# Masks of four attention heads on VectorE, their first inputs loaded earlier, and another share-out of the last additions and stores

## The chip, the cores and the metric

One core of a Trainium2 chip. The metric is the device time of one execution in microseconds, the median of several runs. The core has five engines that each work through their own list of instructions in order: TensorE (PE) multiplies matrices, VectorE (DVE), ScalarE (ACT) and GpSimd (POOL) work on tiles in on-chip memory, and SyncE (SP) issues transfers. ACT and POOL can issue transfers too. All matrices are fp32; a product is made of three passes over "high" and "low" parts (`whi`/`wlo`, `h_hi`/`h_lo`) so that little precision is lost.

## What is computed

One layer of a hybrid decoder for a prompt of 512 tokens with 16 learned ones in front, and for 8 sequences that decode 4 tokens each over 512 cached positions in pages of 128. D_MODEL is 2048, there are 8 heads of 128.

```python
h = rmsnorm(x, g_pre)
q, k, v, ga, cb, cc, ch, gc, ma, mc = split(h @ w_in)
a = stick_breaking(q, k, v) * silu(ga)
u = cc * ch
c = cb * causal_conv(u_ext) * silu(gc)
merged = sigmoid(ma + b_ga) * (a @ w_pa) + sigmoid(mc + b_gc) * (c @ w_pc)
y = x + rmsnorm(merged @ w_out, g_post)

# stick_breaking, per head; mask[t, s] = (s < t)
z = q @ k.T * SCALE + b_sb
log_keep = where(mask, log_sigmoid(-z), 0)
after = reverse_cumsum(log_keep) - log_keep
attn = where(mask, exp(log_sigmoid(z) + after), 0)
out = attn @ v
```

## The kernel before

The work runs in this order: norm and transposes; q, k and v and four heads (0 to 3, `head_now`); the decode scores over the key pages; the other columns of w_in (the "gates" loop over j and w); then the products with w_pc, in a loop over 16 column blocks j, about 1194 to 1350 us; then w_pa (from 1370 us), w_out, and the end (`rows`, `finish`). A weight block arrives by SP's queue as `raw`, ACT casts it to `whi`, DVE makes `wlo`.

Heads 4 to 7 (`head_here`) are attended inside the w_pc loop, at j = 0, 3, 6 and 9, so that their chain of small steps lies between products of w_pc. A head's scores z are computed with keys on partitions, in three groups of tiles (A: 128 x 512, B and C: 128 x 416). For each group ACT makes |z|, Exp, Ln and Relu (`softplus_parts`), DVE adds them up into r (L408 to L411), a mask sets r to 0 where the key isn't before the query, ACT and DVE split r (`hi`/`lo`, L423/L424), and PE adds the sums over later keys onto z (L593: `neg_u` is the triangle of -1, `neg_one` a full block). Then ACT takes Exp (e, L597), e is masked and split, and PE multiplies it by v (L603: `o`). DVE multiplies o by the gate (`gated`, L1034) and it is split into `a_hl`, the input of w_pa.

The masks are POOL instructions (`affine_select`, L550), ten a head: five on r, five on e. POOL also issues transfers in its own order: the value pages of the decode (`vpage`, L636), and in the w_pc loop the store of each gated product (L1064: `gate_scr <- gt`), followed by the loads of those gates for the w_pa stage (L1081: `gt <- gate_scr`). Loads of L1081 reuse the buffers that the stores of L1064 read.

The decode's value products (L747: `tp <- vpage`) are spread by `dec_step` over the gates and the w_pc loop; each is a matmul of 128 x 32 by 128 x 512, for one of four column quarters of a PSUM bank, and behind eight sequences' worth of them come transposes (L755) and additions (L760).

At the end `rows` turns the last columns of w_out into token rows (L1141, L1144), ACT squares them, DVE applies g_post; `finish` makes the factor `rs` and adds og * rs to x: for every row group four pieces of 512 columns, of which DVE does some (L1169), while for the others ACT scales (L1171) and POOL adds (L1172). All stores are SP's (L1174). Row group 4 has 32 rows. `finish` runs twice: for row groups 0 and 1 before the last products, for 2, 3 and 4 behind them.

The order of instructions on each engine is set when the program is built: a scheduler simulates a timeline and places the instructions by it. A change of one engine's work thus moves others.

Of the kernel before, what the change touches and what calls it, by code (L numbers as in the profile page):

```python
# [17 lines left out]
P = 128  # L18
# [34 lines left out]
LNEXP = "natural_log_exp_and_others"  # L53
SCALE = P ** -0.5
GATE_Q, GATE_K, GATE_V, GATE_GA = 0, 1024, 2048, 3072
COL_CB, COL_CC, COL_CH, COL_GC, COL_MA, COL_MC = 4096, 5120, 6144, 7168, 8192, 10240
# [3 lines left out]
def hybrid_step_kernel(  # L60
# [340 lines left out]

    def softplus_parts(e, l, r, t, src, bias, neg_bias=None):

        act.activation(e, src, AF.Abs, bias=bias)
        act.activation(e, e, AF.Exp, scale=-1.0)
        act.activation(l, e, AF.Ln, bias=one_c[:e.shape[0]])
        act.activation(r, src, AF.Relu, bias=bias)
# [3 lines left out]
        dve.tensor_add(r, r, t)  # L411


    d3ctx, hctx, nctx = (ExitStack() for _ in range(3))
    z_all = dp.tile([P, NPG, DB, H, DT], F32, name="z_all")
# [105 lines left out]

    def attend(pl, h, khi, klo, vhi, vlo, qr, pl_a=None):

# [22 lines left out]
        def mask(x, g):  # L546
            for st, c0, n, ts, m in tiles_of(g):
                w = min(st * P + m - ts, n)
                if w > 0:
                    pool.affine_select(out=x[:m, c0:c0 + w], in_=x[:m, c0:c0 + w], pattern=[[1, w]],  # L550
                                       compare_op=ALU.is_gt, fill=0.0, base=ts - st * P, channel_multiplier=-1)

        rs_, sp_, sf_ = {}, {}, {}
        for g in GROUPS:
# [28 lines left out]
        ot = o_ps()  # L583
        dve.memset(ot, 0.0)
        for g in GROUPS:
# [37 lines left out]
    def head_later(h):  # L623
# [3 lines left out]
        dec_step(2, "part")  # L627


    page_reg = {}  # L630
# [7 lines left out]
    def decode_steps():  # L638
# [3 lines left out]
        for said, part in (("part", units[:DEC1]), ("logits", units[DEC1:])):  # L642
            with tc.tile_pool(name="dec1", bufs=2, side="right") as d1:
                for hf, b in part:
# [7 lines left out]
                    for pg in range(NPG):  # L652
# [17 lines left out]
                        yield  # L670
            yield said
        BHT = DB * H * DT

# [54 lines left out]
        for g in range(2):  # L728
            for hf in range(2):
                cs = slice(hf * 512, (hf + 1) * 512)  # L730
                po = t_ps()
                for pg in range(NPG + 1):
                    if pg < NPG:
                        vts = []
                        for j in range(4):
                            vt = d3.tile([P, 512], F32, name="vpage", bufs=8)
                            page_load(vt, vc, 4 * g + j, pg, cs)
                            vts.append(vt)
                        if g + hf + pg == 0:
                            yield "values"  # L740
# [269 lines left out]
    a_hl = tok.tile([P, KD, TQ], F32R, tag="B", name="a_hl")  # L1010
    hl = cctx.enter_context(tc.tile_pool(name="headin", bufs=1))
# [3 lines left out]
    def head_loads(h):  # L1015
        kr = hl.tile([P, T], F32, name="kr")
        nc.sync.dma_start(kr, k_scr[h])
        qr = hl.tile([P, PQ], F32, name="qr")
        nc.sync.dma_start(qr, qt_scr[h][:, 0:PQ])
        vn = hl.tile([P, 5, P], F32, name="vn")  # L1020
        nc.sync.dma_start(vn[:, 0:4, :], vn_scr[h][0:512].rearrange("(a p) d -> p a d", p=P))
        nc.sync.dma_start(vn[0:16, 4, :], vn_scr[h][512:TP])
        return kr, vn, qr

    loaded = head_loads(NOW)
    for k in range(0, 8, 2):
# [15 lines left out]
    def head_here(h):  # L1042
        kr, vn, qr = loaded if h == NOW else head_loads(h)
        ot = attend(cp, h, *k_split(cp, kr), *v_split(cp, vn), qr, cp2)
        gated(h, ot, sg_load(h)[:, 0, 0:PQ])
# [20 lines left out]
    split_evac(a_hl[:, 0:8, PQ:TQ], a_hl[:, 8:16, PQ:TQ], sg_s, sg_s)  # L1066
    d3ctx.close()
    dctx.close()
    cctx.close()
# [50 lines left out]
    with tc.tile_pool(name="outp", bufs=1) as op:  # L1120
        ogr = op.tile([REST, D - CW], F32, name="ogr")

        def og_rest(cs):

            return og_a[:REST, 4 * D + cs.start:4 * D + cs.stop] if cs.stop <= CW else \
                ogr[:, cs.start - CW:cs.stop - CW]

# [8 lines left out]
        def rows(j, ii, tb, g, rest):  # L1136
# [6 lines left out]
            if rest:  # L1143
                pe.transpose(out=pt[:REST, n:n + P], in_=tb[:, ROWS[4][0]:ROWS[4][0] + REST], identity=ident)  # L1144
            for b, i in enumerate(ii):
# [3 lines left out]
            if rest:  # L1149
                square(4, j, pt[:REST, n:n + P], REST)  # L1150
                dve.tensor_mul(og_rest(cs), pt[:REST, n:n + P], g[:REST])

        def finish(ii, npool):

# [4 lines left out]
            with tc.high_priority():  # L1159
                dve.reduce_sum(s1, ssq[:, ii[0]:ii[-1] + 1, :], axis=mybir.AxisListType.X)  # L1160
                rstd_of(dve, rs, s1, tmp, P, w)
            for b, i in enumerate(ii):
                n = ROWS[i][1]
                for c in range(4):
                    cs = slice(c * CW, (c + 1) * CW)
                    og = og4[:n, i, cs] if i < 4 else og_rest(cs)
                    xc, r = xs_[i][:n, cs], rs[:n, b:b + 1]
                    if c < 4 - npool[b]:
                        dve.scalar_tensor_tensor(out=xc, in0=og, scalar=r, in1=xc, op0=ALU.mult, op1=ALU.add)  # L1169
                    else:  # L1170
                        act.activation(og, og, AF.Copy, scale=r)  # L1171
                        pool.tensor_add(xc, xc, og)  # L1172
                    for p0, p1, dst in outs[i]:
                        nc.sync.dma_start(dst[:, cs], xc[p0:p1])  # L1174

# [56 lines left out]
        xa = tok.tile([P, 4, D], F32, tag="A", name="xa")  # L1232
        xs_ += [xa[:, i, :] for i in range(3)]
        parts = [((0, n, xp[t0:min(t0 + n, PQ), :]),) for t0, n in ROWS]
# [3 lines left out]
        outs[3] = ((0, np_, yp[t0:PQ, :]), (np_, P, ys))  # L1238
        for i in range(5):
            load_rows(xs_[i], parts[i])  # L1240

        finish((0, 1), (1, 1))
        both = []
# [3 lines left out]
        for m in range(2):  # L1247
# [4 lines left out]
            rows(j + m, (2, 3), cols[m], g[:, m], True)  # L1252
        finish((2, 3, 4), (1, 1, 2))
    mctx.close()
# [25 lines left out]
```

## Time and profile before

| | |
|---|---|
| median of 3 runs | 1661.16 us (1659.37 to 1664.0) |
| profiled execution | 1663.13 us, its span 1661.5 us |
| PE busy | 1600.6 us (96% of the span) |
| DVE, ACT, POOL busy | 1252.6, 974.8, 262.7 us |
| granted PE clock, mean | 0.981 |

Busy time is the time in which an engine executes an instruction; waits and the issue of transfers are left out. The span is what the profile covers, and the time of that execution is 1.6 us longer. Where PE is busy for nearly all of the span, the places with idle time or with a granted clock below 1 are few, and they are read from windows of 5 us. In a row of the timeline stand the start, the duration, the engine, the line, the operation with what it writes and reads, the count, and in brackets how long the engine had been idle and what ended that.

### The profile page before, as it was taken

The page shows a single profiled execution, that of the slowest core. Times are in us where ns is not written, and L with a number is a line of the kernel's source. Part 1 is how long each engine was busy: PE and PEld are TensorE (multiplying, and loading weights), DVE is VectorE, ACT ScalarE, POOL GpSimd, SP SyncE. Part 2 cuts the span into 40 slices and gives each one's busy share as a digit, 9 for nine tenths or more (in the row PEclk, how much of TensorE's full clock was granted, in tenths as well). Part 3 has the DMA queues.
Part 4 walks back from the last instruction along what each step waited for, and adds up shares of the span by engine and source line. Part 5 has one row for each costly group of instructions (what it writes and reads, how often), then busy time and mean ns, then how long its engine had stood idle before and what let it go on. Part 6 is the DMA issues. An engine that isn't in the chain of part 4 may idle for free. (4 is left out here: it accounts for less than half of the span.)

```text
span 1661.5 us, 31640 instructions
## 1 busy us (share of the span) xinstructions
PE 1600.6 (96%) x12174; PEld 1540.7 (93%) x12174; DVE 1252.6 (75%) x1669; ACT 974.8 (59%) x2532; POOL 262.7 (16%) x460
## 2 busy tenths in 40 slices
PE   7999999999999999999999999899999979999995
PEld 6999999999999999999999999888878969999995
DVE  4538888797979898988878888865466647877775
ACT  6247887746765656565667677953445533445552
POOL 0033233222101010000011011031232210000002
PEclk7999999999999999999999999999999989999998
DMA  9255545435544444444455454355895535433335
GB/s 225 77 177 155 155 144 160 143 119 171 174 131 128 128 134 129 129 133 134 135 157 170 148 166 143 103 185 163 283 317 169 170 99 174 154 111 94 94 105 193
DMA packets 307468, 252.72 MB, mean 152 GB/s; under 512 B 11569, under 2 KB 276853, under 8 KB 306213
## 3 DMA queue, kind: packets, MB, share of 16 engines
q1 hardware_dynamic: 279269, 161.90, 34.0%
q0 software_dynamic: 28016, 88.80, 16.3%
q8 instruction: 95, 1.56, 0.4%
q14 instruction: 56, 0.46, 0.1%
q10 hardware_dynamic: 32, 0.01, 0.0%
HBM read 217.95 MB, written 32.71 MB: 151 GB/s over the span
## 5 line engine op out<-in xcount | busy, mean ns | idle before, releaser
L235 ACT CAST whi<-raw 128x1024 fp32r<-128x1024 f32 x251 | 262.8, 1049 | 259.7 <-PE o L849 74.3
L236 DVE TENSOR_TENSOR wlo<-raw,whi 128x1024 fp32r<-128x1024 f32 x251 | 306.1, 1220 | 75.6 <-ACT whi L235 57.4
L849 PE MATMUL mm<-h_hi,whi 128*128 128x272 f32 (+1 forms) x1152 | 333.9, 290 | 6.2 <-ACT whi L235 6.2
L849 PE MATMUL mm<-h_lo,whi 128*128 128x272 f32 (+1 forms) x1152 | 332.4, 289 | 0.0
L849 PE MATMUL mm<-h_hi,wlo 128*128 128x272 f32 (+1 forms) x1152 | 332.0, 290 | 0.0
L849 PE MATMUL o<-t_hi,whi 128*128 128x272 f32 (+1 forms) x864 | 253.7, 294 | 7.4 <-DVE c L875 3.0
L849 PE MATMUL o<-t_hi,wlo 128*128 128x272 f32 (+1 forms) x864 | 251.2, 291 | 1.3 <-DVE wlo L236 1.3
L849 PE MATMUL o<-t_lo,whi 128*128 128x272 f32 (+1 forms) x864 | 251.2, 291 | 0.0
L236 DVE TENSOR_TENSOR wlo<-s,whi 128x1024 fp32r<-128x1024 f32 x126 | 154.0, 1222 | 101.3 <-ACT whi L235 101.0
L849 PEld LDWEIGHTS mm<-h_hi,whi 128*128 128x128 f32 x1152 | 217.4, 189 | 10.8 <-ACT whi L235 7.8
L849 PEld LDWEIGHTS mm<-h_lo,whi 128*128 128x128 f32 x1152 | 216.8, 188 | 2.5 <-issue 2.5
L849 PEld LDWEIGHTS mm<-h_hi,wlo 128*128 128x128 f32 x1152 | 216.4, 189 | 2.8 <-issue 2.5
L664 ACT ACTIVATE junk<-pr 128x128 f32<-128x128 f32 x592 | 182.7, 309 | 29.2 <-DVE pr L658 13.4
L235 ACT CAST whi<-s 128x1024 fp32r<-128x1024 f32 x126 | 131.6, 1045 | 100.1 <-PE o L849 32.2
L251 PE MATMUL mm<-h_hi,whi 128*128 128x280 f32 (+1 forms) x640 | 187.1, 293 | 0.0
L251 PE MATMUL mm<-h_hi,wlo 128*128 128x280 f32 (+1 forms) x640 | 187.1, 293 | 0.0
L251 PE MATMUL mm<-h_lo,whi 128*128 128x280 f32 (+1 forms) x640 | 186.7, 292 | 0.0
L849 PEld LDWEIGHTS o<-t_hi,whi 128*128 128x128 f32 x864 | 164.2, 190 | 16.5 <-issue 5.0
L849 PEld LDWEIGHTS o<-t_hi,wlo 128*128 128x128 f32 x864 | 164.4, 190 | 2.3 <-DVE wlo L236 2.2
L849 PEld LDWEIGHTS o<-t_lo,whi 128*128 128x128 f32 x864 | 164.9, 191 | 0.0
L658 DVE TENSOR_TENSOR pr<-kpage,qb 128x1024 f32<-128x1024 f32 x128 | 152.2, 1217 | 7.7 <-DMA kpage<-in_cache_k 3.4
L251 PEld LDWEIGHTS mm<-h_hi,whi 128*128 128x128 f32 x640 | 120.5, 188 | 0.7
(384 smaller groups left out, 3436.2 us busy)
## 6 DMA issues: line engine op xcount, KB each, us to landing
raw<-in_w_in SPq DMA_DIRECT2D x192, 512.0 KB, 4.2
kpage<-in_cache_k POOLq DMA_DIRECT2D x64, 256.0 KB, 3.4
qb<-q_scr POOLq DMA_DIRECT2D x32, 512.0 KB, 5.5
vpage<-in_cache_v POOLq DMA_DIRECT2D x64, 256.0 KB, 5.7
raw<-in_w_out SPq DMA_DIRECT2D x32, 512.0 KB, 4.0
gate_scr<-g POOLq DMA_DIRECT2D x32, 272.0 KB, 3.4
gt<-gate_scr POOLq DMA_DIRECT2D x16, 544.0 KB, 4.1
raw<-in_w_pc SPq DMA_DIRECT2D x16, 512.0 KB, 7.2
```

Of the source, the lines that this page charges most:

```text
L235: act.copy(hi, x)
L236: dve.tensor_sub(lo, x, hi.bitcast(F32))
L251: pe.matmul(o, lhsT=w, rhs=r[:, t0:t1], start=(k == 0 and n == 0), stop=(k == nk - 1 and n == 2))
L658: dve.tensor_mul(pr, kt.unsqueeze(1).broadcast_to([P, 2, 512]), qt))
L664: act.activation(junk, pr[:, t, h * P:(h + 1) * P], AF.Copy, accum_out=z_all[:, pg, b, 4 * hf + h, 2 * i + t:2 * i + t + 1])
L849: pe.matmul(o, lhsT=l[:, k, :], rhs=r, start=(start and k == 0 and m == 0), stop=(stop and k == 7 and m == 2), skip_group_check=True)
```

## The change

1. For heads 4 to 7 the masks become DVE instructions: min(x, BIG) times a 0/1 tile `after`, in place. The softplus instructions of the three groups are issued on ACT one group after the other in a fixed order, ahead of the sums. `o` is zeroed on ACT instead of DVE.
2. The inputs of head 4 (kr, qr, vn) are loaded in the gates loop, in a pool of their own; `vpage` has 7 buffers instead of 8.
3. At the end the 32 rows of group 4 lie as a tile of 128 x 512 (four column quarters below one another), their factor is spread over 128 partitions by a small matmul, and all additions are DVE's, mostly in pieces of 1024 columns. Stores alternate between SP's and ACT's queues: 4 in the first `finish` (8 before), 10 in the last (16 before).

```diff
-    def softplus_parts(e, l, r, t, src, bias, neg_bias=None):
-
-        act.activation(e, src, AF.Abs, bias=bias)
...
+    def softplus_acts(e, l, r, src, bias, pin=lambda ins: ins):
+        pin(act.activation(e, src, AF.Abs, bias=bias))
+        pin(act.activation(e, e, AF.Exp, scale=-1.0))
+        pin(act.activation(l, e, AF.Ln, bias=one_c[:e.shape[0]]))
+        pin(act.activation(r, src, AF.Relu, bias=bias))
...
-                if w > 0:
+                if w > 0 and after is not None:
+                    xm = x[:m, c0:c0 + w]
+                    dve.scalar_tensor_tensor(out=xm, in0=xm, scalar=BIG, in1=after[:m, ts - st * P:ts - st * P + w],
+                                             op0=ALU.min, op1=ALU.mult)
+                elif w > 0:
                     pool.affine_select(out=x[:m, c0:c0 + w], in_=x[:m, c0:c0 + w], pattern=[[1, w]],
...
         for g in GROUPS:
-            zt = gt[g]
-            e, l, r, t = tl("e", g), tl("l", g), tl("r", g), tl("lo", g)
-            softplus_parts(e, l, r, t, zt, b)
+            elr[g] = tl("e", g), tl("l", g), tl("r", g)
+            if after is not None:
+                softplus_acts(*elr[g], gt[g], b, pin)
+        for g in GROUPS:
+            (e, l, r), t = elr[g], tl("lo", g)
+            if after is None:
+                softplus_acts(e, l, r, gt[g], b)
+            softplus_sums(e, l, r, t)
             mask(r, g)
...
-        dve.memset(ot, 0.0)
+        if after is None:
+            dve.memset(ot, 0.0)
+        else:
+            act.copy(ot, zero_c.broadcast_to([P, PQ]))
...
-                            vt = d3.tile([P, 512], F32, name="vpage", bufs=8)
+                            vt = d3.tile([P, 512], F32, name="vpage", bufs=7)
...
+            if j + w == 14:
+
+                after = hl[0].tile([P, P], F32, name="after")
+                dve.tensor_scalar_add(after, neg_u.bitcast(F32), 1.0)
+                loaded = head_loads(NOW)
...
-        def finish(ii, npool):
+        def finish(ii, cuts):
...
+            queues = cycle((nc.sync, act))
             for b, i in enumerate(ii):
-                n = ROWS[i][1]
+                if i == 4:
+                    continue
+                for c0, c1 in zip(cuts[b], cuts[b][1:]):
+                    xc = xs_[i][:, c0:c1]
+                    dve.scalar_tensor_tensor(out=xc, in0=og4[:, i, c0:c1], scalar=rs[:, b:b + 1], in1=xc,
+                                             op0=ALU.mult, op1=ALU.add)
+                    p0, p1, dst = outs[i][0]
+                    next(queues).dma_start(dst[:, c0:c1], xc[p0:p1])
...
+            if ii[-1] == 4:
+                r4 = t_ps()[:, 0:1]
+                pe.matmul(r4, lhsT=to4.rearrange("p a b -> p (a b)"), rhs=rs[:REST, w - 1:w], start=True, stop=True)
+                r4s = op.tile([P, 1], F32, name="r4s")
+                act.copy(r4s, r4)
+                dve.scalar_tensor_tensor(out=xs_[4], in0=ogr, scalar=r4s, in1=xs_[4], op0=ALU.mult, op1=ALU.add)
+                dst = outs[4][0][2]
                 for c in range(4):
...
-                    if c < 4 - npool[b]:
-                        dve.scalar_tensor_tensor(out=xc, in0=og, scalar=r, in1=xc, op0=ALU.mult, op1=ALU.add)
-                    else:
-                        act.activation(og, og, AF.Copy, scale=r)
-                        pool.tensor_add(xc, xc, og)
-                    for p0, p1, dst in outs[i]:
-                        nc.sync.dma_start(dst[:, cs], xc[p0:p1])
+                    next(queues).dma_start(dst[:, c * CW:(c + 1) * CW], xs_[4][c * REST:(c + 1) * REST])
...
-        finish((2, 3, 4), (1, 1, 2))
+        finish((2, 3, 4), ((0, D // 2, D), (0, D // 2, 3 * CW, D)))
```

In the order of the instructions this shows at three places. Up to the w_pc loop every engine's order is the same but for a few rows. First POOL at the end of the heads, before (r and e are head 7's; `gt` a gate tile):

```order
L550 AFFINE_SELECT rA<-rA 128x112
L1064 DMA gate_scr<-gt 128x544
L1081 DMA gt<-gate_scr 128x1088 x2
L550 AFFINE_SELECT r<-r 128x128
L550 AFFINE_SELECT r<-r 16x16
L1064 DMA gate_scr<-gt 128x544
L1081 DMA gt<-gate_scr 128x1088
L550 AFFINE_SELECT r<-r 128x128 x2
```

POOL there with the change:

```order
L667 DMA vpage<-in_cache_v 128x512
L1089 DMA gate_scr<-gt 128x544 x9
L1107 DMA gt<-gate_scr 128x1088
L1089 DMA gate_scr<-gt 128x544
L1107 DMA gt<-gate_scr 128x1088
L1089 DMA gate_scr<-gt 128x544
L1107 DMA gt<-gate_scr 128x1088 x14
```

The masks have left the queue, and the gate loads have only gate stores around them. Second, PE at head 7, from the last products onto z to the first products with v, before:

```order
L593 MATMUL z<-lo,neg_u 128x144
L593 MATMUL z<-hi,neg_one 128x16
L593 MATMUL z<-lo,neg_one 128x16
L593 MATMUL z<-e,neg_one 128x400
L603 MATMUL o<-hi,vhi 128x400
L603 MATMUL o<-lo,vhi 128x400
```

PE there with the change (of the rows between `e,neg_one` and `hi,vhi` the last ones are shown; they are 35 matmuls of w_pc, which go on from z's last one):

```order
L252 MATMUL mm<-c_hl,whi 128x272 x2
L252 MATMUL mm<-c_hl,wlo 128x272
L252 MATMUL mm<-c_hl,whi 128x272
L624 MATMUL o<-hi,vhi 128x400
L252 MATMUL mm<-c_hl,whi 128x272
L252 MATMUL mm<-c_hl,wlo 128x272
L252 MATMUL mm<-c_hl,whi 128x272 x2
L252 MATMUL mm<-c_hl,wlo 128x272
L624 MATMUL o<-lo,vhi 128x400
```

Before, the o products follow z's directly and w_pc is used up by then; now products of w_pc stand between them. Third, PE at the decode's value products beside the first head of the loop, before:

```order
L251 MATMUL mm<-c_hl,whi 128x272
L593 MATMUL z<-loA,neg_u 128x512
L251 MATMUL mm<-c_hl,whi 128x272
L755 MATMUL tp<-ident,ob 128x128 x4
L251 MATMUL mm<-c_hl,wlo 128x272
L747 MATMUL tp<-vpage,z_all 32x512 x4
L593 MATMUL z<-hi,neg_u 128x400
```

PE beside the second head of the loop with the change (soon after its first product of `lo` onto z):

```order
L252 MATMUL mm<-c_hl,wlo 128x272
L779 MATMUL tp<-vpage,z_all 32x512
L252 MATMUL mm<-c_hl,whi 128x272
L779 MATMUL tp<-vpage,z_all 32x512
L252 MATMUL mm<-c_hl,whi 128x272
L252 MATMUL mm<-c_hl,wlo 128x272
```

Where four and more value products stood together, many now stand alone between products of w_pc and the steps of a head. Over the whole program the 64 of them form 31 runs before and 39 with the change.

More of the change, by code (lines that the diff above doesn't have):

```diff
@@ L411, in softplus_parts @@
         dve.tensor_add(r, r, t)
-    d3ctx, hctx, nctx = (ExitStack() for _ in range(3))
+    def softplus_parts(e, l, r, t, src, bias):
+        softplus_acts(e, l, r, src, bias)
+        softplus_sums(e, l, r, t)
+    d3ctx, hlctx, hctx, nctx = (ExitStack() for _ in range(4))
+    hl = []
     z_all = dp.tile([P, NPG, DB, H, DT], F32, name="z_all")
@@ L520, in v_proj, with attend @@
         return v_split(pl, vn)
-    def attend(pl, h, khi, klo, vhi, vlo, qr, pl_a=None):
+    def attend(pl, h, khi, klo, vhi, vlo, qr, pl_a=None, after=None):
         qhi = pl.tile([P, T], F32R, name="qhi")
@@ L627, in head_later, with head_loads @@
         dec_step(2, "part")
+    def head_loads(h):
+        kr = hl[0].tile([P, T], F32, name="kr")
+        nc.sync.dma_start(kr, k_scr[h])
+        qr = hl[0].tile([P, PQ], F32, name="qr")
+        nc.sync.dma_start(qr, qt_scr[h][:, 0:PQ])
+        vn = hl[0].tile([P, 5, P], F32, name="vn")
+        nc.sync.dma_start(vn[:, 0:4, :], vn_scr[h][0:512].rearrange("(a p) d -> p a d", p=P))
+        nc.sync.dma_start(vn[0:16, 4, :], vn_scr[h][512:TP])
+        return kr, vn, qr
     page_reg = {}
@@ L671, in decode_steps @@
             yield said
+        hl.append(hlctx.enter_context(tc.tile_pool(name="headin", bufs=1, side="right")))
         BHT = DB * H * DT
@@ L1043, in head_here @@
         kr, vn, qr = loaded if h == NOW else head_loads(h)
-        ot = attend(cp, h, *k_split(cp, kr), *v_split(cp, vn), qr, cp2)
+        ot = attend(cp, h, *k_split(cp, kr), *v_split(cp, vn), qr, cp2, after)
         gated(h, ot, sg_load(h)[:, 0, 0:PQ])
@@ L1067, in hybrid_step_kernel @@
     d3ctx.close()
+    hlctx.close()
     dctx.close()
@@ L1120, in hybrid_step_kernel @@
     with tc.tile_pool(name="outp", bufs=1) as op:
[L1121 to L1126, printed above, removed]
+        ogr = op.tile([P, CW], F32, name="ogr")
+        to4 = op.tile([REST, 4, REST], F32, name="to4")
+        dve.tensor_copy(to4, ident[:REST, :REST].unsqueeze(1).broadcast_to([REST, 4, REST]))
         ssq = og_a[:, 4 * D + CW:4 * D + CW + 5 * KD].rearrange("p (i j) -> p i j", j=KD)
@@ L1143, in rows @@
             if rest:
-                pe.transpose(out=pt[:REST, n:n + P], in_=tb[:, ROWS[4][0]:ROWS[4][0] + REST], identity=ident)
+                pr = t_ps()[:REST, :P]
+                pe.transpose(out=pr, in_=tb[:, ROWS[4][0]:ROWS[4][0] + REST], identity=ident)
             for b, i in enumerate(ii):
@@ L1149, in rows @@
             if rest:
-                square(4, j, pt[:REST, n:n + P], REST)
-                dve.tensor_mul(og_rest(cs), pt[:REST, n:n + P], g[:REST])
-        def finish(ii, npool):
+                square(4, j, pr, REST)
+                r0, c0 = j // 4 * REST, j % 4 * P
+                dve.tensor_mul(ogr[r0:r0 + REST, c0:c0 + P], pr, g[:REST])
+        def finish(ii, cuts):
             w = len(ii)
@@ L1161, in finish @@
                 rstd_of(dve, rs, s1, tmp, P, w)
+            queues = cycle((nc.sync, act))
             for b, i in enumerate(ii):
[L1163 to L1174 removed]
+                if i == 4:
[6 more added lines that the diff above has]
+                    next(queues).dma_start(dst[:, c0:c1], xc[p0:p1])
+                for p0, p1, dst in outs[i][1:]:
+                    next(queues).dma_start(dst, xs_[i][p0:p1])
+            if ii[-1] == 4:
[5 more added lines that the diff above has]
+                dst = outs[4][0][2]
+                for c in range(4):
+                    next(queues).dma_start(dst[:, c * CW:(c + 1) * CW], xs_[4][c * REST:(c + 1) * REST])
         def x_room(tag):
@@ L1232, in hybrid_step_kernel @@
         xa = tok.tile([P, 4, D], F32, tag="A", name="xa")
-        xs_ += [xa[:, i, :] for i in range(3)]
+        xs_ += [xa[:, 0, :], xa[:, 1, :], xa[:, 2, :CW]]
         parts = [((0, n, xp[t0:min(t0 + n, PQ), :]),) for t0, n in ROWS]
@@ L1238, in hybrid_step_kernel @@
         outs[3] = ((0, np_, yp[t0:PQ, :]), (np_, P, ys))
-        for i in range(5):
+        for i in range(4):
             load_rows(xs_[i], parts[i])
-        finish((0, 1), (1, 1))
+        for c in range(4):
+            nc.sync.dma_start(xs_[4][c * REST:(c + 1) * REST], parts[4][0][2][:, c * CW:(c + 1) * CW])
+        finish((0, 1), ((0, D // 2, D),) * 2)
         both = []
```

18 lines of the change are left out of this document (4 added, 14 removed).

## The prediction

> **What bounds the kernel now.** I read the page first, then the waits of PE.
>
> ```profile
> span 1661.5 us, 31640 instructions
> PE 1600.6 (96%) x12174; PEld 1540.7 (93%) x12174; DVE 1252.6 (75%) x1669; ACT 974.8 (59%) x2532; POOL 262.7 (16%) x460
> ```
>
> PE is busy for 96% of the span, so a change can pay in three ways only: it fills one of PE's gaps, it alters what PE executes, or it shortens the stretch behind PE's last product. The waits of PE that this change touches (engine, line, releaser: total us, times, longest):
>
> ```profile
> PE z L593 <- ACT hi L423: 4.6, 1, 4.6
> PE mm L251 <- DVE gt L1063: 3.1, 3, 1.4
> PE o L603 <- ACT hi L423: 1.7, 1, 1.7
> PE mm L251 <- ACT a_hl L423: 1.4, 1, 1.4
> ```
>
> Each is a single stall or a few, so the windows say where they are and what the granted clock (PEclk) does around them:
>
> ```profile
> 1205.00:1210.00 5.00, 3.76 (x32) 2.10 (x30) 2.53 (x7) 1.04 (x2) 1.08 (x2) 1.00 1.12 350
> 1210.00:1215.00 5.00, 4.29 (x34) 4.29 (x35) 2.97 (x8) 2.43 (x5) 3.77 (x7) 1.00 1.02 311
> 1235.00:1240.00 5.00, 3.26 (x23) 1.86 (x22) 3.59 (x11) 0.72 (x2) 1.60 (x3) 1.00 0.99 325
> 1240.00:1245.00 5.00, 5.00 (x28) 4.52 (x27) 3.36 (x8) 2.08 (x5) 1.63 (x5) 0.66 0.83 282
> 1305.00:1310.00 5.00, 4.53 (x32) 3.88 (x31) 4.17 (x8) 2.10 (x3) 1.66 (x2) 1.00 0.64 204
> 1350.00:1355.00 5.00, 1.75 (x14) 1.53 (x13) 0.00 (x0) 0.00 (x0) 0.36 (x1) 1.00 0.24 92
> 1355.00:1360.00 5.00, 3.04 (x10) 2.04 (x10) 2.58 (x6) 1.54 (x3) 0.73 (x3) 0.60 0.34 111
> 1360.00:1365.00 5.00, 3.30 (x10) 1.93 (x9) 1.63 (x3) 3.17 (x6) 1.26 (x5) 0.50 0.00 0
> 1365.00:1370.00 5.00, 3.69 (x13) 2.84 (x12) 0.76 (x2) 0.56 (x1) 0.00 (x0) 0.50 0.00 0
> 1370.00:1375.00 5.00, 4.88 (x28) 4.89 (x29) 3.98 (x8) 1.53 (x3) 0.55 (x1) 0.69 0.38 115
> ```
>
> The second number is PE's busy time, the third from the end its clock. The end of head 7 (1350 to 1375) loses 3.25 + 1.96 + 1.70 + 1.31 + 0.12 = 8.3 us to idle time, and a clock below 1 loses more of the busy time: 3.04 x 0.40 + 3.30 x 0.50 + 3.69 x 0.50 + 4.88 x 0.31 = 6.2 us. Together 14.5 us. The heads' beginning (1205 to 1245) and 1305 lose 1.24 + 0.71 + 1.74 + 0.47 = 4.2 us idle and 5.00 x 0.34 = 1.7 us of clock: 5.9 us.
>
> The timeline names the cause of the large one:
>
> ```profile
> 1346.42 0.57 POOL L1064 DMA_DIRECT2D gate_scr<-gt  x1
> 1348.60 0.59 DVE L411 TENSOR_TENSOR r<-r,lo 128x416 f32<-128x416 f32 x1
> 1354.64 0.54 POOL L1081 DMA_DIRECT2D gt<-gate_scr  x1 [7.65 <-issue]
> 1355.18 0.56 POOL L550 TENSOR_SCALAR_AFFINE_SELECT r<-r 128x128 f32<-128x128 f32 x2
> 1355.77 0.54 ACT L423 CAST hi<-r 128x416 fp32r<-128x416 f32 x1 [8.74 <-POOL r L550]
> 1356.36 0.59 PE L593 MATMUL z<-hi,neg_u 128*128 128x272 f32 x1 [4.62 <-ACT hi L423]
> ```
>
> Head 7's last r is summed by 1349.19, but its mask is a POOL instruction and stands behind a gate load, which POOL issues only when the store of 1346.42 has landed. The mask so comes 6 us late, PE idles, and from there to 1370 the head runs as a bare chain with nothing between, the clock at half.
>
> **The change part by part.** *Masks on DVE, softplus of the three groups together.* All masks of heads 4 to 7 leave POOL. POOL's order then ends with gate stores and loads alone; the load's wait for landing stays, but no head stands behind it. On PE, products of w_pc now lie between head 7's steps: by the order 35 between its last z and the first o product. The window below gives 5.00/42 = 0.12 us for one, so 4.2 us of cover.
>
> ```profile
> 1375.00:1380.00 5.00, 5.00 (x42) 5.00 (x42) 4.51 (x10) 2.54 (x4) 0.00 (x0) 1.00 0.42 118
> ```
>
> That step's wait was 1.7 us with nothing in between but Exp, mask and cast. The other steps of head 7 have 4 to 65 products ahead of them, and the head has no a_hl wait left, since products of heads 0 to 6 stand in front of head 7's. I take 14.0 of the 14.5 us as gained; the ends are 0 (a new wait as long takes its place) and 14.5.
>
> The masks are work for DVE, ten a head. No such operation on DVE is in the trace. The nearest rows are DVE's small adds and its page-wide second product:
>
> ```profile
> L570 DVE TENSOR_TENSOR r<-r x24: 154/309/443, 153.5 to 1357.5; 16x16 f32<-16x16 f32 x8, 128x144 f32<-128x144 f32 x8, 128x272 f32<-128x272 f32 x8
> 1275.00:1315.00 40.00, 39.53 (x295) 37.57 (x294) 29.25 (x60) 20.56 (x35) 10.77 (x16) 1.00 0.56 167
> ```
>
> 128x128 lies between 16x16 (0.154) and 128x144 (0.31), so ten cost 1.5 to 3.1 us; I take 2.6, as eight of the ten are near the upper size. A head takes about 38 us in which DVE (the fourth number, 29.25 of 40) has some 10 us free, and the zeroing of o moves to ACT, which is freer still: 0 on the path, with 0 to 2.6 x 4 = 10.4 us as bounds. If that cover fails, the late thing is the wlo of a weight block, for which PE's products wait.
>
> *First inputs in the gates, 7 page buffers.* Head 4's three loads move ahead of the last w_in loads on SP's queue. The first two early waits hang on other things:
>
> ```profile
> 1208.24 0.69 DVE L1034 TENSOR_TENSOR sg<-sg 128x512 f32<-128x512 f32 x1 [0.95 <-DMA sg<-a_scr]
> 1236.34 0.42 DVE L760 TENSOR_TENSOR sg_s<-tp,sg_s 128x16 f32<-128x16 f32 x4 [3.80 <-PE tp L755]
> DMA to landing us min/median/max: 3.0/5.9/7.6
> ```
>
> At 1208 DVE waits for a gate row while the DMA engines are full (share 1.12 above): fewer loads there help a little. At 1236 DVE stood 3.8 us for the decode's transposes and then had its r sums in front of gt; by the new order the decode steps lie elsewhere. I take 3 of the 5.9 us as gained, with 0 and 5.9 as ends. The last line is the landing of the value pages (1195 to 1280): with 7 buffers a page comes 0.54 to issue + 5.9 after a buffer falls free; by the order the tightest reuse (after the run of six) leaves about 6 us, so 0, at worst 7.6 + 0.54 - 6 = 2 us.
>
> *Value products in smaller groups.* This is what the new order costs. Each is 32 columns wide, four to a bank:
>
> ```profile
> 1236.86 1.06 PE L747 MATMUL tp<-vpage,z_all 128*32 128x512 f32 x8 [0.43 <-PE mm L251]
> 1237.86 0.45 PE L593 MATMUL z<-hi,neg_u 128*128 128x400 f32 x1
> 1246.84 1.05 PE L747 MATMUL tp<-vpage,z_all 128*32 128x512 f32 x2
> 1247.82 0.39 PE L251 MATMUL mm<-c_hl,whi 128*128 128x272 f32 x1
> ```
>
> Two records are one instruction. Four instructions in a row hold PE for 1237.86 - 1236.86 = 1.00 us, a single one for 1247.82 - 1246.84 = 0.98. So PE pays by the run of up to four. Counted that way over all 64 pages, the order before has 36 groups and the one after 45: nine more, 9 x 0.98 = +8.8 us, all inside a stretch where PE is otherwise full. The ends: 0 if they fall into waits, 8.8 if none does; I take 8.8, by the rows. (The Trainium skill, "TensorE: Matmul & The Clock Gate", Part 3, says that small matmuls run side by side only when they hit different column groups of the array; the rows agree, and by that rule the change pays for each group it breaks, the same +8.8.)
>
> *The end.* The factor rs is ready at 1647.5, and the order of the last products, squares and of rs is the same.
>
> ```profile
> 1647.36 0.16 DVE L136 TENSOR_TENSOR rs<-rtmp 128x3 f32<-128x3 f32 x1
> L1169 DVE SCALAR_TENSOR_TENSOR xa<-og_a,rs,xa x7: 733/1743/1756, 1647.6 to 1655.6; 128x512 f32<-128x512 f32 x6, 32x512 f32<-32x512 f32 x1
> 1656.23 0.73 DVE L1169 SCALAR_TENSOR_TENSOR xa<-ogr,rs,xa 32x512 f32<-32x512 f32 x1
> L1172 POOL TENSOR_TENSOR xa<-xa,og_a x2: 1703/1720/1736, 1648.4 to 1650.1; 128x512 f32<-128x512 f32 x2
> L1174 SPq DMA_DIRECT2D out<-xa x16: 316/372/446, 1648.3 to 1658.9; - x16
> L204 DVE SCALAR_TENSOR_TENSOR hn<-xt,rs,g_bc x10: 1272/1280/1286, 9.4 to 49.8; 128x1024 f32<-128x1024 f32 x8, 48x1024 f32<-48x1024 f32 x2
> 1636.00:1641.00 5.00, 4.53 (x37) 4.38 (x36) 3.31 (x5) 1.48 (x7) 0.82 (x1) 1.00 1.01 379
> ```
>
> A DVE piece takes 0.73 us alone and 1.74 next to POOL's additions. Without those: three of 128x1024 at 1.28, two of 128x512 at 0.74 and the last, with row group 4 as 128 x 512, 0.73: 3.84 + 1.48 + 0.73 = 6.05, from 1647.55 to 1653.6 (before: 1656.96). The four stores behind it, two a queue, start by 1654.1; before, the last issue started at 1658.9 and the span ended 2.6 later. So 1654.1 + 2.6 = 1656.7: 4.8 us. Bytes bound it too: 2.25 row groups of 128 x 2048 floats are 2.36 MB, which at the 379 GB/s of the window take 6.2 us; the first store starts at 1647.55 + 1.28 = 1648.8, so the last byte comes no earlier than 1655.0, and with the landing behind it that is about the same end. On one queue the four last stores would start up to 0.45 apart: 1653.6 + 3 x 0.45 + 2.6 = 1657.55, a gain of 3.9. The ends are 2 (the bytes go at two thirds of that rate) and 6. (The Trainium skill, "DMA: Bandwidth & Descriptors", section "Issuing engines are not separate DMA queues", holds that issuing from several engines saves only the time on the sequencer. That speaks against the second queue; by it the gain would lie between these 3.9 and 4.8 us, and the additions carry most of it.)
>
> **Sum**, against the profiled run, 1663.1 us with a span of 1661.5: -14.0 - 3.0 + 0 + 8.8 - 4.8 = -13.0, so 1650.1. That run lies 2.0 above the median of the runs (1661.2), so I predict 1648.
>
> **The rivals.** *A: the small groups cost nothing* (they fall where PE would have waited for a cast of the head). For it: the order puts many of them between head steps. Against it: w_pc products stand between the same steps, and PE's idle time at that place before was only 4.2 us. It gives 1648 - 8 = 1640. *B: the head's waits come back half.* The masks make head steps longer on DVE, in order behind weight splits of 1.2 us, and the products placed between were placed for other durations. If half of the 17 us stays: 1648 + 8.5 = 1656.5, just below the line of no change. Against it: 35 products stand ahead of the step that waited. *C, slower: DVE becomes the bound of the heads.* If wlo of w_pc blocks comes late behind the masks, PE waits in each head, and a wait was followed by half clock at 1240, which doubles the price: a wait w costs some 2w. It ends above no change from 13/(4 x 2) = 1.6 us a head on; at the whole 2.6 us of masks a head the sum is 1648 + 4 x 5.2 = 1669. Against it: 10 us a head free on DVE. *D: the idle time merely moves* to other waits of the heads, and only the half clock (6.2) and the end are saved: 1661.2 - 6.2 - 4.8 + 8.8 = 1659.0. For it: a chain of waits was removed at one place, and the scheduler shared its slack out over all four heads.
>
> **How the numbers follow.** My forecast 1648 (1643 to 1654) 0.62; A 1640 0.14; B 1656.5 0.10; D 1659 0.07; C 0.07. 0.3% is 5 us, about what a measurement of this kernel can tell from no change, so faster means below 1656.2. Faster holds the forecast, A and half of B: 0.81; the same holds the other half of B and D: 0.12; slower C: 0.07. The range reaches from A's 1640 to 1657, over B: what it leaves out is C, D and the lower half of A, some 0.2.
>
> **What would show it.** Right: PE busy without a break and at clock 1.00 from 1340 to 1375; no POOL select after head 3; a tail of 6 us on DVE with pieces of 1.28 and 0.74; vpage runs of one that hold PE 0.98 each. Wrong: PE waits at z or o products of heads 4 to 7 for a DVE mask or an ACT cast, or a wait for wlo in w_pc; a clock below 1 between 1200 and 1370; DVE pieces of the end above 1.3 us; waits of the value products for a page's landing.

## The result, and the profile after

The changed kernel takes 1648.59 us (median of 7 runs, 1646.35 to 1655.38), the kernel before beside it 1662.28 us (7 runs, 1659.37 to 1665.49). The ratio is 0.9924, 95% interval 0.9905 to 0.9943. The forecast was 1648, from 1640 to 1657, with "faster" as the likeliest.

The profiled execution has a span of 1647.0 us, 14.5 less than before. PE is busy as long as before (it was 1600.6 us), in a shorter span; below, less time at half clock and more groups of value products turn out to cancel:

```profile
span 1647.0 us, 31583 instructions
PE 1600.9 (97%) x12176; PEld 1535.1 (93%) x12176; DVE 1253.7 (76%) x1703; ACT 973.6 (59%) x2531; POOL 232.0 (14%) x414
```

The windows at the places that had lost time (columns as in the prediction: length, busy PE, PEld, DVE, ACT, POOL, then PE's clock, DMA share and GB/s):

```profile
1205.00:1210.00 5.00, 5.00 (x42) 4.88 (x41) 3.22 (x10) 0.72 (x2) 0.54 (x1) 1.00 1.12 332
1235.00:1240.00 5.00, 5.00 (x25) 2.56 (x23) 0.86 (x4) 2.53 (x5) 1.28 (x3) 1.00 0.71 236
1350.00:1355.00 5.00, 5.00 (x39) 4.87 (x39) 2.89 (x4) 1.57 (x2) 0.54 (x1) 1.00 0.15 58
1360.00:1365.00 5.00, 5.00 (x42) 5.00 (x41) 2.66 (x6) 0.89 (x1) 0.00 (x0) 1.00 0.51 156
```

In all 46 windows of 5 us from 1150 to 1380 PE is busy for 5.00 us at clock 1.00: all 20.4 us that the kernel before lost there (12.5 idle, 7.9 to the clock) are gone. But PE has more to do in that stretch, since a value product that stands alone holds it as long as four did (timeline of PE: start, duration, then the next row's start):

```profile
1226.32 1.05 PE L779 MATMUL tp<-vpage,z_all 128*32 128x512 f32 x2
1227.29 0.39 PE L252 MATMUL mm<-c_hl,whi 128*128 128x272 f32 x1
1229.12 1.05 PE L779 MATMUL tp<-vpage,z_all 128*32 128x512 f32 x2
1230.09 0.39 PE L614 MATMUL z<-hi,neg_u 128*128 128x272 f32 x1
```

0.97 us each here, 0.98 in the trace of before; nine groups more are 8.8 us by the latter (ten more in the w_pc loop, one fewer ahead of it). The masks on DVE, by form (the numbers are shortest, median and longest in ns):

```profile
L559 DVE SCALAR_TENSOR_TENSOR r<-r,after x16: 155/284/292, 1215.8 to 1333.2; 128x128 f32<-128x128 f32 x12, 16x16 f32<-16x16 f32 x4
L559 DVE SCALAR_TENSOR_TENSOR rA<-rA,after x4: 268/268/269, 1223.9 to 1335.8; 128x112 f32<-128x112 f32 x4
```

Per head that is 6 x 0.285 + 2 x 0.155 + 2 x 0.27 = 2.6 us. The end, by lines and windows of 1 us:

```profile
1635.07 0.16 DVE L137 TENSOR_TENSOR rs<-rtmp 128x3 f32<-128x3 f32 x1
1635.32 5.00 DVE L1194 SCALAR_TENSOR_TENSOR xa<-og_a,rs,xa 128x1024 f32<-128x1024 f32 x5
1640.24 0.75 DVE L1205 SCALAR_TENSOR_TENSOR xa<-ogr,r4s,xa 128x512 f32<-128x512 f32 x1
```

```profile
1639.00:1640.00 1.00, 0.00 (x0) 0.00 (x0) 1.00 (x3) 0.00 (x0) 0.00 (x0) 0.50 1.03 410
1641.00:1642.00 1.00, 0.00 (x0) 0.00 (x0) 0.00 (x0) 0.00 (x0) 0.00 (x0) 0.50 0.89 283
1642.00:1643.00 1.00, 0.00 (x0) 0.00 (x0) 0.00 (x0) 0.00 (x0) 0.00 (x0) 0.50 0.98 268
1644.00:1645.00 1.00, 0.00 (x0) 0.00 (x0) 0.00 (x0) 0.00 (x0) 0.00 (x0) 0.50 0.61 213
```

DVE is done by 1640.99, 5.8 us behind rs (9.4 before). Yet the span ends 1647.0 - 1635.23 = 11.8 us behind rs, where it was 1661.5 - 1647.52 = 14.0: only 2.2 us less. From 1640 on the DMA engines are busy but move 210 to 290 GB/s, not the 400 of the first pieces.

The account: -20.4 + 8.8 - 2.2 = -13.8 of the -14.5; 0.7 is left over. It doesn't stem from the time ahead of the loop: the first product of w_pc starts at 1193.9 for 1194.7 before, but the one group fewer ahead of it, which the 8.8 already counts, is worth more than that.

### The profile page after: what moved, and what is told of

It reads as the page before. It is cut to its first block, busy times and chain, and to the rows that moved or that the text cites. A ratio compares the mean times of both kernels' runs of the same rounds, so it can differ in the third digit from the quotient of the medians.

```text
span 1647.0 us, 31583 instructions
## 1 busy us (share of the span) xinstructions
PE 1600.9 (97%) x12176; PEld 1535.1 (93%) x12176; DVE 1253.7 (76%) x1703; ACT 973.6 (59%) x2531; POOL 232.0 (14%) x414
## 4 chain that ended last, share of the span: by engine, by line
PE 78%; DVE 5%; ACT 5%; DMA 3%; issue 2%; POOL 0%; DVEq 0%; ACTq 0%; POOLq 0%; SPq 0%
PE mm L252 25%; PE mm L881 24%; PE o L881 20%; PE tp L779 3%; ACT junk L695 2%; ACT whi L236 2%; DMA raw<-in_w_in 2%; DVE pr L689 1%; PE z L614 1%; PE o L624 1%; DVE wlo L237 1%; PE z L545 1%; PE z L881 1%; DMA kpage<-in_cache_k 1%; PE z L1165 0%
## 5 line engine op out<-in xcount | busy, mean ns | idle before, releaser
L881 PEld LDWEIGHTS mm<-h_hi,whi 128*128 128x128 f32 x1152 | 217.5, 189 | 11.9 <-ACT whi L236 8.9
```

The lines of the kernel that those rows point to most:

```text
L881: pe.matmul(o, lhsT=l[:, k, :], rhs=r, start=(start and k == 0 and m == 0), stop=(stop and k == 7 and m == 2), skip_group_check=True)
```

## The experiments

The time of each is set against the kernel before by its ratio, which can be compared from chip to chip (the changed kernel: 0.9924).

**1. Value products in whole groups, with a barrier.** The four products of a page group in one critical section:

```diff
+                    with tc.tile_critical():
                         for j in range(4):
```

> The changed kernel with the four value products of a page group kept together, so that the order has 20 groups in place of 45. Theory (every group holds PE for 0.98 us, alone or four together): 25 groups fewer are -24.5 us of PE, and as the heads keep their cover the time falls to about 1625. Rival 1 (single products cost nothing, since they lie where PE would wait anyway): no change, 1646 to 1651. Rival 2 (a whole group waits for its last page and PE stands still): the -24.5 is eaten by waits of value products for vpage, 1635 to 1660, and the waits show it.

Measured: 1701.78 us, ratio 1.0244 (1.0205 to 1.0284). None of the three; it is 42 us slower than the kernel before (1659.45 beside it). The section is more than a grouping: PE stands still ahead of it until transfers and steps have come, most of which have nothing to do with it (some of the waits of PE: total us, times, longest).

```profile
PE tp L780 <- DMA raw<-in_w_pc: 10.3, 2, 6.5
PE tp L780 <- DMA gate_scr<-gt: 5.2, 1, 5.2
PE tp L780 <- DMA vpage<-in_cache_v: 4.9, 1, 4.9
PE tp L780 <- DMA qr<-qt_scr: 2.5, 1, 2.5
```

```profile
1200.00:1250.00 50.00, 35.06 (x224) 28.60 (x224) 18.13 (x33) 17.00 (x28) 9.29 (x17) 0.80 0.69 219
```

From 1150 to 1380 PE was idle for 43.9 us and lost 28.3 more to the clock. These losses hide the groups' price, so the time alone says nothing on it.

**2. The same grouping by order alone.** The pages of a group are loaded in reverse, and the products keep their written order on PE, so that the first product waits for the page that comes last and the other three can follow at once:

```diff
-                        for j in range(4):
+                        for j in (3, 2, 1, 0):
                             vt = d3.tile([P, 512], F32, name="vpage", bufs=7)
...
-                            vts.append(vt)
+                            vts.insert(0, vt)
...
-                        pe.matmul(po[32 * j:32 * (j + 1), :], lhsT=lhs, rhs=rhs, start=(pg == 0),
+                        pin(pe.matmul(po[32 * j:32 * (j + 1), :], lhsT=lhs, rhs=rhs, start=(pg == 0),
```

> The changed kernel with the value products held in their written order on PE and the last page of each group loaded first, so that the four of a group come together: 20 groups in place of 45, without the barrier of the run before this one, in which everything around a group stood still. Theory (a group holds PE for 0.98 us, alone or four together): -24.5 us, less up to 8 us of waits for a last page, so 1624 to 1633. Rival 1 (single products cost nothing): 1646 to 1651. Rival 2 (a group that waits for its last page stops PE, with half clock behind it): no gain, 1640 to 1660, and the waits of PE show vpage.

Measured: 1626.99 us, ratio 0.9795 (0.9761 to 0.9829). The theory holds, both rivals fall. The span is 1625.4: 21.6 less for 25 groups less. PE's waits in the stretch are few, and none is for a page:

```profile
PE mm L252 <- DVE gt L1088: 3.4, 2, 3.2
PE tp L779 <- issue: 1.3, 1, 1.3
```

**3. Early inputs undone.** Head 4's loads at the start of the w_pc loop, `vpage` with 8 buffers:

```diff
-            if j + w == 14:
-                after = hl[0].tile([P, P], F32, name="after")
-                dve.tensor_scalar_add(after, neg_u.bitcast(F32), 1.0)
-                loaded = head_loads(NOW)
...
+    after = hl[0].tile([P, P], F32, name="after")
+    dve.tensor_scalar_add(after, neg_u.bitcast(F32), 1.0)
+    loaded = head_loads(NOW)
```

> The changed kernel with head 4's inputs loaded where they were before (at the start of the w_pc loop) and 8 page buffers; the order then has 35 groups of value products in place of 45. Theory (groups cost 0.98 us each, the early loads remove waits of about 3 to 6 us at 1205 to 1245): -9.8 + 3 to 6 us, so 1642 to 1646. Rival (groups cost nothing and the early loads are what counts): +3 to +6 us, 1651 to 1655.

Measured: 1643.79 us, ratio 0.9908 (0.9881 to 0.9936), span 1641.2. The theory's range holds: the median is 4.8 us below the changed kernel's although waits return. (The intervals of the two ratios overlap, so that it is faster than the changed kernel is likely, not shown.)

```profile
1205.00:1210.00 5.00, 3.58 (x30) 2.14 (x30) 3.49 (x10) 2.42 (x5) 2.64 (x5) 1.00 1.09 303
1350.00:1355.00 5.00, 3.48 (x17) 2.78 (x16) 2.85 (x6) 1.66 (x2) 0.54 (x1) 0.83 0.12 21
```

Idle time and clock lose 6.1 us, some at 1205, where the early loads were meant to act, and 3.0 at the end of the heads: head 4's first z product starts at 1215.0 in place of 1204.4, and no w_pc product is left between head 7's last z and its first o, where the changed kernel has 35. Ten groups less bring 9.8.

**4. That kernel with whole groups.** The edit of 2 on the kernel of 3.

> The same grouping in the kernel with head 4's inputs loaded in the w_pc loop and 8 page buffers: 20 groups in place of 35. Theory: 15 x 0.98 = 14.7 us less than that kernel's 1643.8, so 1629, up to 6 us more if pages are waited for. Rival (the grouping delays pages and the heads wait again): 1640 to 1650.

Measured: 1629.31 us, ratio 0.9817 (0.9785 to 0.9848). As the theory has it: 15 groups less, 14.5 us less than 3. Waits for gt (5.4 us in all) are what it has in place of 3's waits.

**5. Masks on POOL again.**

```diff
-                if w > 0 and after is not None:
+                if False:
```

> The changed kernel with the masks of heads 4 to 7 on POOL again, all else kept. Theory (what cost the time was the mask that stood behind a gate load on POOL): by the order head 7's masks of r now stand ahead of the gate loads but its masks of e behind two of them, so a wait of PE returns at the o products of head 7 alone, +2 to +10 us with half clock, 1651 to 1659. Rival (the softplus at one go and its place among the w_pc products is what counts, masks on either engine do): no wait returns, 1646 to 1651.

Measured: 1649.59 us, ratio 0.9941 (0.9922 to 0.9961). In its time the rival holds. The wait at the o products that the theory named does return, but it is 0.6 us, not 2 to 10:

```profile
1205.00:1210.00 5.00, 3.17 (x23) 2.84 (x22) 3.18 (x7) 0.62 (x1) 0.00 (x0) 1.00 1.05 334
1350.00:1355.00 5.00, 4.36 (x32) 3.86 (x30) 1.14 (x3) 2.75 (x6) 1.80 (x6) 1.00 0.44 147
```

2.5 us of loss in all where the kernel before has 20.4, and 1.8 of them are a wait for gt at 1205, which 9 has too, with its masks on DVE. With head 7's steps placed elsewhere, its masks of r stand ahead of the gate loads on POOL too. So the stall of before was a matter of the order on POOL's queue, and another engine for the masks was one way out, not the only one.

**6. Only the masks on DVE, in the kernel before.** The same edit of `mask`, with `after` made at the start of the w_pc loop.

> The kernel before with the masks of heads 4 to 7 on DVE, nothing else. By the order no mask stands behind a gate load any more and there are 35 groups of value products for 36. Theory (the end of the heads lost 14.5 us to the mask in POOL's queue): 14 to 15 us less than before, about 1646, while the early waits of 1205 to 1245 stay. Rival (the masks alone leave the head a bare chain at its end, since softplus at one go is what spreads its steps): at most half of it, 1652 to 1660.

Measured: 1651.62 us, ratio 0.9950 (0.9932 to 0.9968). A little below the rival's range and far from the theory's 1646, and by the windows it is the rival's mechanism:

```profile
1205.00:1210.00 5.00, 3.23 (x28) 2.54 (x21) 3.07 (x6) 2.42 (x5) 4.10 (x8) 1.00 1.10 309
1235.00:1240.00 5.00, 1.87 (x7) 1.47 (x8) 2.94 (x8) 1.21 (x3) 2.56 (x5) 0.88 0.87 290
1240.00:1245.00 5.00, 5.00 (x26) 3.91 (x26) 1.80 (x5) 1.61 (x3) 0.10 (x2) 0.78 0.37 123
1345.00:1350.00 5.00, 4.89 (x36) 4.28 (x34) 2.94 (x8) 2.06 (x5) 0.00 (x0) 1.00 0.33 113
1350.00:1355.00 5.00, 3.41 (x11) 2.58 (x12) 2.48 (x7) 2.49 (x5) 0.00 (x0) 0.65 0.00 2
1355.00:1360.00 5.00, 3.57 (x13) 2.75 (x13) 1.48 (x3) 0.62 (x1) 0.53 (x1) 0.50 0.00 0
1360.00:1365.00 5.00, 5.00 (x36) 5.00 (x35) 4.35 (x10) 2.31 (x3) 0.00 (x0) 0.83 0.44 135
```

```profile
PE o L608 <- ACT hi L424: 1.7, 1, 1.7
PE mm L252 <- ACT a_hl L424: 1.4, 1, 1.4
```

The wait of 4.62 us for the mask is gone, but head 7 still ends as a bare chain at half clock, with the same 1.7 and 1.4 us of waits as before. From 1345 to 1365 idle time and clock lose 0.11 + 1.59 + 1.43 + 3.41 x 0.35 + 3.57 x 0.50 + 5.00 x 0.17 = 7.0 us, half of the 14.5. The early waits are still there.

**7. No fixed order on ACT.**

```diff
-                softplus_acts(*elr[g], gt[g], b, pin)
+                softplus_acts(*elr[g], gt[g], b)
```

> The changed kernel without the fixed order of the softplus instructions of the three groups on ACT (they are still issued ahead of the sums). Theory (the head's waits went because its steps have w_pc products between them, which the scheduler places whatever ACT's order): no wait of the heads comes back, 44 groups in place of 45, 1645 to 1651. Rival (the fixed order is what lets the three groups follow each other): waits of z products for ACT return in some heads, 1652 to 1660.

Measured: 1647.62 us, ratio 0.9922 (0.9897 to 0.9947): the same as with it. No wait of the heads comes back (0.03 us in all). So what the "one go" does doesn't come from the fixed order; that it comes from where the instructions stand in the program is what is left, and was not tried by itself.

**8. The whole groups in the kernel before.** The edit of 2, nothing else.

> The kernel before with the value products in whole groups (20 in place of 36), nothing else. Theory: 16 x 0.98 = 15.7 us of PE less; the stall of the heads' end stays or moves with the order, so 1645, from 1643 to 1652. Rival (only where the heads have cover does the grouping pay; here PE waits instead): 1655 to 1662.

Measured: 1633.89 us, ratio 0.9839 (0.9802 to 0.9877): 26 us faster than before, more than the range. The losses from 1150 to 1380 fell too, to 15.8 from 20.4, but the end of the heads is still bare:

```profile
1335.00:1340.00 5.00, 3.02 (x11) 1.98 (x10) 1.80 (x3) 3.03 (x6) 1.26 (x5) 0.78 0.00 2
1340.00:1345.00 5.00, 3.56 (x12) 2.75 (x13) 1.38 (x2) 0.62 (x1) 0.00 (x0) 0.50 0.00 0
```

So 16 groups (15.7 us) and 4.6 us of losses explain 20.3 of the profiled run's 25.5 (1661.5 - 1636.0); the other 5.2 lie outside the stretch and the end (below).

**9. The old end on the changed kernel.** The code from `rows` to the last `finish` as before.

> The changed kernel with the end of the kernel before (additions shared with POOL, 16 stores on SP). Theory (from the two traces the end behind rs takes 14.0 us before and 11.8 with the change): 2.2 us slower than the changed kernel, 1651. Rival (the 4.8 us of the prediction, with the rest hidden in the profiled execution): 1653 to 1654.

Measured: 1652.06 us, ratio 0.9950 (0.9932 to 0.9968). It is slower than the changed kernel by 0.0026 of 1662, that is 4 us, with both intervals 3 us wide on either side: this can't tell 2.2 from 4.8. The profile can: its end behind rs takes 14.0 us, as in the kernel before, and 2.0 us were lost to a wait for gt at 1205, though up to there PE, ACT, POOL and SP work in the changed kernel's order: this wait differs by that much between executions.

**10. One store queue.**

```diff
-            queues = cycle((nc.sync, act))
+            queues = cycle((nc.sync,))
```

> The changed kernel with all stores of both finishes on SP's queue. In the changed kernel the end behind rs took 11.8 us in place of the 9.2 forecast, and from 1640 on two queues in flight moved 270 GB/s at a DMA share of 1.0, where one queue before had moved 370 to 400. Theory A (the interleaving of two queues slows the DMA engines): with one queue the rate stays near 390 and the end comes 1 to 2 us earlier, 1647. Theory B (the rate falls since the last pieces are 2 KB rows or 32 partitions, whatever the queue): the end stays or comes up to 1 us later for the issues, 1649.

Measured: 1648.32 us, ratio 0.9934 (0.9908 to 0.9960); the end behind rs takes 11.7 us. Theory B: the rate falls on one queue just as on two, and the second queue is worth nothing.

```profile
1639.00:1640.00 1.00, 0.00 (x0) 0.00 (x0) 1.00 (x3) 0.00 (x0) 0.00 (x0) 0.50 1.00 401
1642.00:1643.00 1.00, 0.00 (x0) 0.00 (x0) 0.00 (x0) 0.00 (x0) 0.00 (x0) 0.50 1.08 311
1643.00:1644.00 1.00, 0.00 (x0) 0.00 (x0) 0.00 (x0) 0.00 (x0) 0.00 (x0) 0.50 0.87 275
```

(The section of the Trainium skill that the prediction weighed, "Issuing engines are not separate DMA queues" in "DMA: Bandwidth & Descriptors", says that several issuing engines save only the time it takes to issue; the two ends agree with it, 11.74 us with one queue and 11.77 with two, so that even this saving does not show.)

**11. Row group 4 in one store.**

```diff
-                for c in range(4):
-                    next(queues).dma_start(dst[:, c * CW:(c + 1) * CW], xs_[4][c * REST:(c + 1) * REST])
+                next(queues).dma_start(dst.rearrange("r (c w) -> c r w", c=4), xs_[4])
```

> The changed kernel with row group 4 stored by one issue from 128 partitions in place of four from 32 each. In the changed kernel the four last issues took 0.6 to 1.5 us each and the rate was 270 GB/s at a DMA share of 1.0. Theory A (pieces of 32 partitions slow the DMA engines): the rate stays near 390 and the end behind rs is 1 to 1.5 us shorter than 11.8. Theory B (the 2.4 MB keep the engines full until 1645 whatever the last pieces are): within 0.4 us of 11.8.

Measured: 1652.24 us, ratio 0.9959 (0.9942 to 0.9975). Neither theory: the end takes 14.9 us. The store runs long after the others, at a quarter of the DMA engines:

```profile
1642.00:1643.00 1.00, 0.00 (x0) 0.00 (x0) 0.18 (x1) 0.00 (x0) 0.00 (x0) 0.50 0.94 289
1646.00:1647.00 1.00, 0.00 (x0) 0.00 (x0) 0.00 (x0) 0.00 (x0) 0.00 (x0) 0.50 0.25 25
1648.00:1649.00 1.00, 0.00 (x0) 0.00 (x0) 0.00 (x0) 0.00 (x0) 0.00 (x0) 0.50 0.23 88
```

Its target's outermost dimension has four steps, and the share is 0.25. (The Trainium skill, "DMA: Bandwidth & Descriptors", section "Rules for kernel authors", states that an outermost dimension of c below 16 keeps a transfer to at most c engines; the rows agree, 4 of 16.) The rate before that store is as low as in the changed kernel, so the four pieces of 32 partitions aren't what lowers it.

**12. Whole groups with a new end.** The edits of 2 and 11, and a first piece of 512 columns.

> The changed kernel with whole groups of value products, one store of row group 4, and the first piece of the last additions cut to 512 columns so that the first store starts 0.5 us earlier. Theory: the whole groups' 1627 less 0.5 to 2 us of the end, 1625 to 1626.5. Rival (the end is bound by bytes and gains nothing): 1627.

Measured: 1629.53 us, ratio 0.9819 (0.9789 to 0.9850). Neither holds: the edit of 11 costs here too, and the end takes 15.6 us, 3.9 more than in 2. The lowest median is that of 2, 1626.99.

**All runs together.** If the reading is right, the span is a constant plus the time lost from 1150 to 1380, plus 0.98 us a group, plus the end behind rs. All numbers are of the profiled executions, in us; losses are read from windows of 5 us as in the prediction, groups from the order. Run 1 is left out: it lost 72.3 us from 1150 to 1380 and, unlike the others, 10.0 more from 1100 to 1150; with both taken off, its rest is 1587.6.

| kernel | span | lost | groups | end | rest |
|---|---|---|---|---|---|
| before | 1661.5 | 20.4 | 36 | 14.0 | 1591.8 |
| changed | 1647.0 | 0.0 | 45 | 11.8 | 1591.1 |
| 2, whole groups | 1625.4 | 6.4 | 20 | 11.7 | 1587.7 |
| 3, early inputs undone | 1641.2 | 6.1 | 35 | 11.7 | 1589.1 |
| 4, both | 1627.1 | 7.2 | 20 | 11.7 | 1588.6 |
| 5, masks on POOL | 1649.9 | 2.5 | 45 | 11.8 | 1591.5 |
| 6, masks on DVE alone | 1649.9 | 14.2 | 35 | 14.0 | 1587.4 |
| 7, no fixed order | 1641.9 | 0.0 | 44 | 11.9 | 1586.9 |
| 8, groups in before | 1636.0 | 15.8 | 20 | 14.0 | 1586.6 |
| 9, old end | 1650.4 | 2.0 | 45 | 14.0 | 1590.3 |
| 10, one queue | 1647.1 | 0.0 | 45 | 11.7 | 1591.3 |
| 11, group 4 in one store | 1651.3 | 0.9 | 45 | 14.9 | 1591.4 |
| 12, whole groups, new end | 1628.4 | 4.1 | 20 | 15.6 | 1589.1 |

The spans differ by 36 us, the rest by 5.2. So the three terms carry the differences. The 5 us lie ahead of the w_pc loop: the start of the first w_pc product, less 0.98 us for each group ahead of it, runs from 1170.8 to 1175.5 us in these kernels, and what is left of the rest behind it differs by 1.6. In 7 that product starts 4.5 us sooner than in the changed kernel (1189.4 for 1193.9), though every engine's order is the same up to there: so it is a difference between executions, not between kernels. What makes it was not tried.

## Why the prediction was right, step by step

- *The end of the heads, 14.0 forecast*: 14.5 came. The time was right. That the mask behind a gate load set off the stall is borne out: with the mask away (6), the wait of 4.6 us is away. But the prediction put two things into this one term, the masks' move and the w_pc products between head 7's steps, and did not say what each is worth; 6 shows that the masks' move alone leaves 7.0 us. With the softplus in one go and `o` zeroed on ACT as well (3), 3.0 are left; with the early inputs besides (the changed kernel), 0, and there w_pc products stand between head 7's steps. 5 shows that with these, the masks may as well stay on POOL: 0.6 us.
- *Products as cover, 4.2 us against a wait of 1.7*: right; no wait is left at z or o.
- *Early waits, 3 of 5.9*: too small, all 5.9 went, though part of that is luck: 5, 9 and 11 have the early loads too and lost 1.8, 2.0 and 0.9 us there. The undoing (3) brings back 3 us there and 3 at the end of the heads, where the prediction had not looked for them.
- *Masks on DVE, 2.6 us a head, hidden*: measured 2.6, and no wait came from them. Rival C falls.
- *Seven page buffers, 0 to 2 us*: no wait for a page in the changed kernel; 0. But the groups are the price of this part of the change: with the early loads and the seven buffers undone together (3), 45 become 35, 9.8 us less against 6.1 us of losses more. By these sums the second part of the change costs 3.7 us; which of its two halves breaks the groups was not tried.
- *Value products, +8.8*: right, and the largest gain that the runs found beyond the change: 2, 4 and 8 each gain by the group. Rival A falls: the table fits with 0.98 us for every group, alone or not. (The 36 and 45 groups, and the 31 and 39 runs, count the products of the new tokens beside the 64 of the pages.)
- *The end, 4.8 forecast*: 2.2 came. The additions were sized rightly (DVE done 5.8 us behind rs, forecast 6.05). The step that failed is that of the bytes: 2.36 MB at the 379 GB/s of an earlier window. That rate holds for the first pieces of 128 rows; for what follows the windows show 210 to 290 GB/s at a DMA share near 1. The step that let the last stores land 2.6 us behind the start of the last issue fails with it, since a queue stood ahead of them: the last issue starts 6.5 us behind rs, as forecast, and the span ends 5.3 us after that. 10 excludes the two queues as the cause and 11 the small last pieces. That leaves the pieces of row group 3, which go out as 96 and 32 rows. The packets in the changed kernel's trace point there: those of 4 KB took about 0.165 us in the pieces of 128 rows and 0.21 to 0.25 us in the piece of 96. Why they take longer no run tried.
- That the sum came out within 1 us of the median is partly luck: the end was forecast 2.6 us too good, the early waits 2.9 and the end of the heads 0.5 too bad, and 0.7 is left over. This turns the sum of 1650.1 into the 1648.6 that was measured; the forecast of 1648 then came close because it took off 2.0 us for the profiled run of the kernel before.

Rivals B and D fall with the windows: none of the waits moved to another place.

## What to carry to other kernels

A scheduler that fills gaps with small work can break up instructions that were cheap only together: count the groups in the order, not the instructions, and price each group from the trace; here 25 groups (24.5 us) were worth more than every loss that the change removed (20.4). Work that is moved elsewhere can break such groups: here the early loads, with one page buffer less, did, and by the sums cost more than they gained. A stall in a chain has two parts, the late step and the bare chain behind it; here moving the late step to another engine cured the first, and it took other work between the steps to cure the second. For an end that is bound by stores, take the rate from pieces of the same shape, not from the best window.

## What was not expected of the hardware

- A store of 128 partitions whose target has an outermost dimension of four ran at a DMA share of 0.25 and took the end from 11.8 to 14.9 us, though it replaced four issues by one.
- The rate of stores fell from 400 to some 280 GB/s at a DMA share that stayed near 1 (0.87 to 1.08 until 1644), on one queue as on two.
- Not every wait of PE costs clock: 1.8 us of idle time at 1205 left it at 1.00 (5), 3.1 us at 1235 took it to 0.88 and then 0.78 (6).
